# A U stage in 512-column matmuls, gelu's last product on GpSimd, and expert lists made by one-hot products

## The chip, the cores and the metric

The kernel runs on one core of one Trainium2 chip. The metric is the device time of one execution in microseconds (us). The kernel before took 2601.82 us, the median of three runs (2600.1 to 2602.65). Engines are named as in the profile: PE is TensorE, DVE is VectorE, ACT is ScalarE, POOL is GpSimd, SP issues most loads.

## The reference

Two transformer blocks run one after the other on 256 tokens of width 2048, in float32. The change touches the first block's expert layer alone, which looks up experts by product keys:

```python
v1, i1 = lax.top_k(s1, 16)                    # scores of 128 keys, for 8 heads, two sides
v2, i2 = lax.top_k(s2, 16)
vs, ci = lax.top_k(v1[..., :, None] + v2[..., None, :], 16)
eidx = e1 * 128 + e2                          # 128 of 16384 experts for each token
gates = softmax(vs)
act = gelu(einsum('tkd,td->tk', expert_u[eidx], x))
out = einsum('tk,tkd->td', act * gates, expert_v[eidx])
```

`expert_u` and `expert_v` are 16384 x 2048 each.

## The kernel before

It is one program, unrolled, in which each engine takes its instructions in the order in which they are written; semaphores between engines come from the use of the tiles. A stream of steps feeds PE (`Stream`); each step has a `prep` (load, split, one step ahead: `la = 1`) and an `mm` (its matmuls). Beside it runs a list of generators, the background: after each step it may spend a budget (2.2 a step, and 2.0 from step 64 on), and each `yield` of a generator says what its piece costs. So the place of background work in each engine's queue is set by these numbers.

A float32 product with nearly full precision is made of three products of a faster type, fp32r: an operand is split into a high part (a copy on ACT) and a low part (a subtraction, source minus high part, on DVE), and high x high, high x low and low x high are summed in PSUM.

*U stage (128 steps, lines 776 to 851).* Step f takes 128 experts and computes their products with all 256 tokens, whether a token chose them or not. Their rows of `expert_u` are loaded, transposed in blocks on DVE (`turn`, L808), and used as weights against x, held transposed in sixteen blocks k of 128 rows: `xt["h"]` and `xt["l"]`, the high and low parts, with 256 columns (tokens) each. In steps 0 to 63 the blocks k = 0 to 7 are done as plain float32 products (L829, weights `uT`, moving `xf`), which come first in the step, and k = 8 to 15 in three fp32r products of 256 columns each (L834, L835, L836); from step 64 on all sixteen blocks are done in three. The high parts are made by ACT at L818, the low parts by DVE at L823, in tiles of 1024 columns, four of each kind.

The result is 128 experts x 256 tokens in PSUM. gelu without its half (which lies in the gates) follows: Square on ACT (L839), a product on DVE (L840), and one step later, in `u_finish`, Tanh on ACT (L849), a product with the PSUM values on DVE (L850), and the write to the DRAM table `AG` from GpSimd's queue (L851).

*Background of the U stage.* The scores and the two rounds of top-k (DVE, about steps 3 to 21, 31 to 41 and 51 to 67), the gates of each token as products of two one-hot matrices (PE, ACT and DVE, L1048 to L1065), which GpSimd's queue writes into the other half of `AG` (L1082), and `lists_gen`. That sorts the 16384 experts into four classes: chosen in the first 128 tokens only, in both halves, in the second half only, in none. It computes the place of each expert in the sorted list, as integers `posU`, and then 128 indirect DMAs on GpSimd write the expert numbers to these places of a DRAM table `listD` (L1121, each with a small memset behind it, five in a yield of 2.0). The table is read back, transposed by PE (L1134) and copied to `listI` (L1135).

*V stage.* Steps of 128 list entries gather rows of `AG` and of `expert_v` by `listI` (L872, L873), multiply activations and gates, split both and multiply on PE (L896 to L898), for one or both halves of the tokens. Where the classes begin and end in steps is fixed by `WA, WB0, WB1`: the blocks from WB0 to WA count for both halves. A flag is set where the classes don't fit these bounds; then further blocks run behind a branch.

Of the kernel before, what the change touches and what calls it, by code (L numbers as in the profile page):

```python
# [12 lines left out]
F32 = mybir.dt.float32  # L13
# [5 lines left out]
OP = mybir.AluOpType  # L19
# [10 lines left out]
WA, WB0, WB1 = 82, 27, 111  # L30
# [59 lines left out]
def tile_kernel(ctx: ExitStack, tc: tile.TileContext, A, out, dbg=None):  # L90
# [20 lines left out]
    def bank(tag):  # L111
        return psp.tile([128, 512], F32, tag=tag, name=tag)
# [156 lines left out]

    def new_xt():  # L270
        xt["h"] = xp.tile([128, 16, 256], F32R, tag="xh", name="xh")
        xt["l"] = xp.tile([128, 16, 256], F32R, tag="xl", name="xl")
# [30 lines left out]
    def flat(t):  # L303
        return t.rearrange("p a b -> p (a b)")
# [446 lines left out]
    listD = dr.tile([NE * 128, 64], F32, name="listD")  # L751
# [10 lines left out]
    r_bc = tk.tile([128, 256], F32, name="r_bc")  # L762
# [17 lines left out]
    gap = tk.tile([1, 1], F32, name="gap")  # L780
# [6 lines left out]
    class UStep:  # L787
# [23 lines left out]
        def prep(self):  # L811
            if self.uT is None:
                self.turn()
            n = (16 - self.nf) * 128 // self.nw
            self.u = []
            for i in range(self.nw):
                hi, lo = wh_tile()[:, :n], wl_tile()[:, :n]
                S.activation(hi, self.uT[:, self.nf * 128 + i * n:self.nf * 128 + (i + 1) * n], AF.Copy)  # L818
                self.u.append((hi, lo))
            if self.f + 1 < NE:  # L820
                steps[self.f + 1].turn()
            for i, (hi, lo) in enumerate(self.u):
                V.tensor_tensor(lo, self.uT[:, self.nf * 128 + i * n:self.nf * 128 + (i + 1) * n], hi.bitcast(F32),  # L823
                                op=OP.subtract)

        def mm(self):
            acc = ubank[self.f % 3][:, 0:256]
            for k in range(self.nf):
                T.matmul(acc, self.uT[:, k * 128:(k + 1) * 128], xf[:, k, :], start=(k == 0), stop=False)  # L829
            per = (16 - self.nf) // self.nw  # L830
# [14 lines left out]
    def u_finish():  # L845
        if not pend:
            return
        f, x, a = pend.pop()
        S.activation(a, a, AF.Tanh, scale=GC3)  # L849
        V.scalar_tensor_tensor(a, a, 1.0, x, op0=OP.add, op1=OP.mult)  # L850
        G.dma_start(AG[f * 128:f * 128 + 128, 0:256], a)  # L851

    class VStep:
# [12 lines left out]
        def prep(self):  # L866
# [12 lines left out]
            for c in range(2):  # L879
                if self.rest:  # L880
                    hi, lo = [xt[n].rearrange("p k t -> p (k t)")[:, c * 1024:(c + 1) * 1024] for n in "hl"]
# [203 lines left out]
    def lists_gen():  # L1085
# [27 lines left out]
        V.tensor_copy(posU, pf[:, 0:128])  # L1113
# [6 lines left out]
        for f in range(NE):  # L1120
            i = G.indirect_dma_start(out=listD[:, :], out_offset=bass.IndirectOffsetOnAxis(ap=posU[:, f:f + 1], axis=0),  # L1121
                                     in_=idf[:, f:f + 64], in_offset=None)
            tc.declare_no_dep(i.ins, group="list", reason="the rows written are all different")
            tc.add_to_no_dep_group("list", i.ins)
# [422 lines left out]
    def merged_gen(i, j0, j1):  # L1547
        for j in range(j0, j1):
# [7 lines left out]
            split(flat(xt["h"][:, k0:k0 + 2, :]), flat(xt["l"][:, k0:k0 + 2, :]), pt)  # L1556
# [39 lines left out]
```

## Time and profile before

| | us |
|---|---|
| median of three runs | 2601.82 |
| the profiled execution's own time | 2613.04 |
| its span, first to last instruction | 2611.3 |
| U stage, first to last U matmul | 391.3 to 1343.7 |
| of it, lists and scatters | 1076.4 to 1343.7 |
| first V product | 1357.29 |

The span is what the views below cover; the time has a little around it. The page's busy shares are means over all stages, so what an engine does in one stage is read from windows.

### The profile page before, as it was taken

How to read it: one execution, taken by the hardware profiler on the slowest of the kernel's cores; microseconds unless marked ns; L12 is line 12 of the kernel's file. 1: busy time of each engine (PE TensorE's matmuls, PEld its weight loads, DVE VectorE, ACT ScalarE, POOL GpSimd, SP SyncE). 2: the span in 40 equal slices, each digit the busy share in tenths (PEclk: the TensorE clock that was granted, in tenths of full speed). 3: DMA queues.
4: the chain of work that ended last, by engine and by line, in shares of the span. 5: the costliest groups of instructions: out<-in, count | busy, mean ns of one | idle time of the engine just before them, and what ended most of it. 6: DMA issues, size and time to landing. Idle time of an engine off the chain costs nothing. (4 is left out here: it accounts for less than half of the span.)

```text
span 2611.3 us, 38031 instructions
## 1 busy us (share of the span) xinstructions
PE 2516.7 (96%) x13895; PEld 2195.1 (84%) x13896; DVE 1815.7 (70%) x2804; ACT 1315.0 (50%) x2169; POOL 554.3 (21%) x789
## 2 busy tenths in 40 slices
PE   9999989999999999998779999999999999999999
PEld 8877779899898999997668888887888888888887
DVE  5665678987979989886447777777665456754564
ACT  6764643254452577543235555555555456544443
POOL 3000000001201112388725555553000000000000
PEclk9999999999999999999789999999999999999999
DMA  6644876565757868696469989987555545555554
GB/s 220 193 129 146 193 165 167 165 168 168 220 144 201 212 176 223 181 241 192 127 241 324 320 321 318 320 317 273 189 191 187 184 163 180 190 178 193 181 193 157
DMA packets 251619, 538.63 MB, mean 206 GB/s; under 512 B 29800, under 2 KB 165952, under 8 KB 236832
## 3 DMA queue, kind: packets, MB, share of 16 engines
q1 hardware_dynamic: 206864, 344.54, 44.4%
q0 software_dynamic: 40992, 189.67, 21.2%
q10 hardware_dynamic: 3568, 1.91, 0.3%
q8 instruction: 111, 1.82, 0.3%
q14 instruction: 84, 0.69, 0.1%
HBM read 494.06 MB, written 41.94 MB: 205 GB/s over the span
## 5 line engine op out<-in xcount | busy, mean ns | idle before, releaser
L120 DVE TENSOR_TENSOR wl<-raw,wh 128x1024 fp32r<-128x1024 f32 (+4 forms) x642 | 740.3, 1171 | 375.8 <-ACT wh L119 341.3
L119 ACT ACTIVATE wh<-raw 128x1024 fp32r<-128x1024 f32 (+4 forms) x642 | 640.1, 1011 | 372.2 <-PE acc L247 279.0
L836 PE MATMUL acc<-xh,wl 128*128 128x256 f32 x1536 | 444.7, 289 | 31.0 <-DVE wl L823 20.7
L245 PE MATMUL acc<-wh,xh 128*128 128x512 f32 (+2 forms) x1152 | 456.7, 396 | 6.0 <-ACT h L406 4.2
L834 PE MATMUL acc<-xh,wh 128*128 128x256 f32 x1536 | 456.0, 297 | 6.1 <-issue 5.5
L835 PE MATMUL acc<-xl,wh 128*128 128x256 f32 x1536 | 441.6, 288 | 9.3 <-issue 8.5
L247 PE MATMUL acc<-wh,xl 128*128 128x512 f32 (+2 forms) x1152 | 447.3, 388 | 0.0
L246 PE MATMUL acc<-wl,xh 128*128 128x512 f32 (+2 forms) x1152 | 446.6, 388 | 0.3 <-DVE wl L120 0.3
L808 DVE STREAM_TRANSPOSE uT<-raw 128x2048 f32<-128x2048 f32 x128 | 295.4, 2308 | 60.5 <-PE acc L829 54.0
L836 PEld LDWEIGHTS acc<-xh,wl 128*128 128x128 f32 x1536 | 300.5, 196 | 39.2 <-DVE wl L823 26.0
L835 PEld LDWEIGHTS acc<-xl,wh 128*128 128x128 f32 x1536 | 301.2, 196 | 11.9 <-issue 10.2
L834 PEld LDWEIGHTS acc<-xh,wh 128*128 128x128 f32 x1536 | 300.9, 196 | 11.8 <-issue 9.9
L245 PEld LDWEIGHTS acc<-wh,xh 128*128 128x128 f32 x1152 | 217.5, 189 | 47.3 <-ACT h L406 4.6
L839 ACT ACTIVATE ga<-acc 128x256 f32<-128x256 f32 x128 | 49.1, 383 | 412.3 <-PE acc L836 325.0
L247 PEld LDWEIGHTS acc<-wh,xl 128*128 128x128 f32 x1152 | 217.3, 189 | 44.0
L246 PEld LDWEIGHTS acc<-wl,xh 128*128 128x128 f32 x1152 | 217.8, 189 | 41.0 <-DVE wl L120 0.7
L818 ACT ACTIVATE wh<-uT 128x1024 fp32r<-128x1024 f32 x192 | 195.1, 1049 | 87.3 <-DVE uT L808 87.2
L829 PE MATMUL acc<-xf,uT 128*128 128x256 f32 x1024 | 234.3, 382 | 3.9 <-ACT h L404 3.9
L823 DVE TENSOR_TENSOR wl<-uT,wh 128x1024 fp32r<-128x1024 f32 x192 | 224.6, 1197 | 7.6 <-ACT wh L818 7.5
L851 POOL DMA_DIRECT2D AG<-ga x128 | 71.1, 556 | 739.4 <-DVE ga L850 723.7
L829 PEld LDWEIGHTS acc<-xf,uT 128*128 128x128 f32 x1024 | 190.9, 191 | 28.2 <-ACT h L404 4.3
L872 POOL DMA_INDIRECT ag<-AG,listI x111 | 142.5, 1284 | 75.9 <-DVE pl L120 51.6
(418 smaller groups left out, 3817.4 us busy)
## 6 DMA issues: line engine op xcount, KB each, us to landing
raw<-in_expert_u_dram SPq DMA_DIRECT2D x1024, 128.0 KB
raw<-in_w_in_dram SPq DMA_DIRECT2D x96, 1024.0 KB
raw<-in_w_out_dram SPq DMA_DIRECT2D x32, 1024.0 KB
raw<-in_w_pq_dram SPq DMA_DIRECT2D x64, 256.0 KB
AG<-ga POOLq DMA_DIRECT2D x128, 128.0 KB
AG<-GB POOLq DMA_DIRECT2D x64, 256.0 KB
raw<-in_w_ple_gate_dram SPq DMA_DIRECT2D x16, 1024.0 KB
raw<-in_w_in_dram SPq DMA_DIRECT2D x16, 544.0 KB
```

What stands on the lines that cost most here:

```text
L119: S.activation(hi, src, AF.Copy)
L120: V.tensor_tensor(lo, src, hi.bitcast(F32), op=OP.subtract)
L245: T.matmul(o, xh, hi, start=first, stop=False)
L246: T.matmul(o, xh, lo, start=False, stop=False)
L247: T.matmul(o, xl, hi, start=False, stop=last)
L808: V.transpose(uT.rearrange("p b g j -> p g b j"), self.raw.rearrange("p g (b i) -> p g b i", i=32))
L818: S.activation(hi, self.uT[:, self.nf * 128 + i * n:self.nf * 128 + (i + 1) * n], AF.Copy)
L823: V.tensor_tensor(lo, self.uT[:, self.nf * 128 + i * n:self.nf * 128 + (i + 1) * n], hi.bitcast(F32), op=OP.subtract)
L829: T.matmul(acc, self.uT[:, k * 128:(k + 1) * 128], xf[:, k, :], start=(k == 0), stop=False)
L834: T.matmul(acc, hi[:, c], xt["h"][:, k, :], start=(k == 0), stop=False)
L835: T.matmul(acc, hi[:, c], xt["l"][:, k, :], start=False, stop=False)
L836: T.matmul(acc, lo[:, c], xt["h"][:, k, :], start=False, stop=(k == 15))
```

## The change

It has four parts.

1. *U in 512 columns.* The tiles `xh` and `xl` no longer hold the high and the low parts, but the blocks 0 to 7 and 8 to 15, each with high and low part side by side. One matmul of 512 columns then multiplies a high weight block with both; its bank holds two sums, which a copy on ACT and an add on DVE put together. The order within a step is: all high blocks but the last, the float32 blocks, the low blocks, the last high block.
2. *GpSimd* subtracts the last quarter of a step's low parts, and makes gelu's last step, an add of 1 and a product, in SBUF.
3. *The lists* are made without DRAM: the list is a sum, over 128 groups of 128 experts, of products of two one-hot matrices (low seven bits of the place against high seven bits, with the expert's number as the value), in 16 groups of eight. A few small products make the part of the number that the group contributes.
4. `WA, WB0, WB1` go from 82, 27, 111 to 81, 28, 110. The pool `t1` has seven buffers instead of five; `r_bc` lies in the pool `g2`.

PE at the start of the U stage. Names on the left of the arrow are outputs; `wh` and `wl` are high and low weights. Before:

```order
L829 MATMUL acc<-xf,uT 128x256 x8
L834 MATMUL acc<-xh,wh 128x256
L835 MATMUL acc<-xl,wh 128x256
L836 MATMUL acc<-xh,wl 128x256
L834 MATMUL acc<-xh,wh 128x256
```

and now (x8 joins the last high block of one step with the seven first ones of the next):

```order
L846 MATMUL acc<-xl,wh 128x512 x7
L852 MATMUL acc<-xf,uT 128x256 x8
L854 MATMUL acc<-xl,wl 128x256 x8
L846 MATMUL acc<-xl,wh 128x512 x8
L852 MATMUL acc<-xf,uT 128x256 x8
```

The float32 blocks and the low blocks have moved behind the high ones.

DVE in a U step of the first half, with a piece of top-k (`oh`, `e`) behind it. Before:

```order
L808 STREAM_TRANSPOSE uT<-raw 128x4x16x32
L823 TENSOR_TENSOR wl<-uT,wh 128x1024
L850 SCALAR_TENSOR_TENSOR ga<-ga,acc 128x256
L840 SCALAR_TENSOR_TENSOR ga<-ga,acc 128x256
L1017 TENSOR_TENSOR oh<-rf,iota 128x512
L1019 TENSOR_TENSOR oh<-oh,i_2672 128x512
```

and now:

```order
L814 STREAM_TRANSPOSE uT<-raw 128x4x16x32
L834 TENSOR_TENSOR wl<-uT,wh 128x768
L859 TENSOR_TENSOR gx<-acc,gx 128x256
L862 SCALAR_TENSOR_TENSOR ga<-ga,gx 128x256
L1041 TENSOR_TENSOR oh<-rf,iota 128x512
L1043 TENSOR_TENSOR oh<-oh,i_2672 128x512
```

The product for the step before (L850) is gone from DVE; the add (L859) stands directly ahead of the product (L862) that takes the square of the add's result, `ga`, from ACT.

GpSimd where the lists are made. Before:

```order
L1125 MEMSET gap 1x1
L851 DMA AG<-ga 128x256
L1082 DMA AG<-GB 128x8x64
L1121 DMA listD<-idf,posU 16384x64
L1125 MEMSET gap 1x1
```

and now:

```order
L1106 DMA AG<-GB 128x8x64
L828 TENSOR_TENSOR wl<-uT,wh 128x512
L872 TENSOR_SCALAR ga<-ga 128x256
L873 TENSOR_TENSOR ga<-ga,gx 128x256
L874 DMA AG<-ga 128x256
```

The scatters are gone, and each step has three operations of arithmetic ahead of its write.

The diff, cut to its core:

```diff
-WA, WB0, WB1 = 82, 27, 111
+WA, WB0, WB1 = 81, 28, 110
...
     def new_xt():
-        xt["h"] = xp.tile([128, 16, 256], F32R, tag="xh", name="xh")
-        xt["l"] = xp.tile([128, 16, 256], F32R, tag="xl", name="xl")
+        xt["x"] = [xp.tile([128, 8, 2, 256], F32R, tag=t, name=t) for t in ("xh", "xl")]
+        xt["h"], xt["l"] = Half(xt["x"], 0), Half(xt["x"], 1)
...
     def t1(dt, name):
-        return tk.tile([128, 256], dt, tag="t1", name=name, bufs=5)
+        return tk.tile([128, 256], dt, tag="t1", name=name, bufs=7)
...
                 S.activation(hi, self.uT[:, self.nf * 128 + i * n:self.nf * 128 + (i + 1) * n], AF.Copy)
                 self.u.append((hi, lo))
+            q = n * (4 - self.nw) // 4
+            hi, lo = self.u[-1]
+            G.tensor_tensor(lo[:, q:], self.uT[:, 2048 - n + q:], hi[:, q:].bitcast(F32), op=OP.subtract)
             if self.f + 1 < NE:
                 steps[self.f + 1].turn()
             for i, (hi, lo) in enumerate(self.u):
-                V.tensor_tensor(lo, self.uT[:, self.nf * 128 + i * n:self.nf * 128 + (i + 1) * n], hi.bitcast(F32),
-                                op=OP.subtract)
+                src = self.uT[:, self.nf * 128 + i * n:self.nf * 128 + (i + 1) * n]
+                m = n if i + 1 < self.nw else n * (4 - self.nw) // 4
+                V.tensor_tensor(lo[:, :m], src[:, :m], hi[:, :m].bitcast(F32), op=OP.subtract)
 
         def mm(self):
-            acc = ubank[self.f % 3][:, 0:256]
+            bank = ubank[self.f % 3]
+            acc = bank[:, 0:256]
...
+            def high(k):
+                T.matmul(bank, part(k, 0), xt["x"][k // 8][:, k % 8].rearrange("p n t -> p (n t)"),
+                         start=(k == self.nf), stop=(k == 15))
+
+            for k in range(self.nf, 15):
+                high(k)
             for k in range(self.nf):
-                T.matmul(acc, self.uT[:, k * 128:(k + 1) * 128], xf[:, k, :], start=(k == 0), stop=False)
...
+                T.matmul(acc, self.uT[:, k * 128:(k + 1) * 128], xf[:, k, :], start=False, stop=False)
             for k in range(self.nf, 16):
-                hi, lo = self.u[(k - self.nf) // per]
-                c = slice((k - self.nf) % per * 128, ((k - self.nf) % per + 1) * 128)
-                T.matmul(acc, hi[:, c], xt["h"][:, k, :], start=(k == 0), stop=False)
-                T.matmul(acc, hi[:, c], xt["l"][:, k, :], start=False, stop=False)
-                T.matmul(acc, lo[:, c], xt["h"][:, k, :], start=False, stop=(k == 15))
+                T.matmul(acc, part(k, 1), xt["h"][:, k, :], start=False, stop=False)
+            high(15)
             u_finish()
+            u = t1(F32, "gx")
+            S.activation(u, bank[:, 256:512], AF.Copy)
+            V.tensor_tensor(u, acc, u, op=OP.add)
             a = t1(F32, "ga")
-            S.activation(a, acc, AF.Square)
-            V.scalar_tensor_tensor(a, a, GC1 / GC3, acc, op0=OP.add, op1=OP.mult)
-            pend.append((self.f, acc, a))
+            S.activation(a, u, AF.Square)
+            V.scalar_tensor_tensor(a, a, GC1 / GC3, u, op0=OP.add, op1=OP.mult)
+            pend.append((self.f, u, a))
...
         S.activation(a, a, AF.Tanh, scale=GC3)
-        V.scalar_tensor_tensor(a, a, 1.0, x, op0=OP.add, op1=OP.mult)
+        G.tensor_scalar(a, a, 1.0, None, op0=OP.add)
+        G.tensor_tensor(a, a, u, op=OP.mult)
         G.dma_start(AG[f * 128:f * 128 + 128, 0:256], a)
...
         yield 3.0
-        for f in range(NE):
-            i = G.indirect_dma_start(out=listD[:, :], out_offset=bass.IndirectOffsetOnAxis(ap=posU[:, f:f + 1], axis=0),
-                                     in_=idf[:, f:f + 64], in_offset=None)
...
-            G.memset(gap, 0.0)
-            if f % 5 == 4:
-                yield 2.0
-        lt = t1(F32, "lt")
-        G.dma_start(GB, listD.rearrange("(b p) o -> b p o", p=128))
-        for _ in range(4):
-            yield 2.0
-        V.tensor_copy(lt[:, 0:128], GB[:, :, 0])
-        pt = bank("ms")
-        T.transpose(pt[:, 0:128], lt[:, 0:128], ident)
-        V.tensor_copy(listI, pt[:, 0:128])
...
+        def hots(tag, col, n):
+            o = tk.tile([128, 8, 128], BF16, tag=tag, name=tag, bufs=3)
+            V.tensor_tensor(o[:, 0:n], iotaf[:, None, :].to_broadcast([128, n, 128]),
+                            pq[:, col:col + n][:, :, None].to_broadcast([128, n, 128]), op=OP.is_equal)
+            return o
...
+        def products(f0, oa, ob):
+            for j in range(8):
+                T.matmul(lst, ob[:, j], oa[:, j], start=(f0 + j == 0), stop=(f0 + j == NE - 1))
+
+        for f0 in range(0, NE, 8):
+            oa, ob = hots("o1", f0, 8), hots("o2", 128 + f0, 8)
+            S.activation(flat(oa), flat(oa), AF.Copy, scale=pcol)
+            if prev:
+                products(*prev)
+            prev = (f0, oa, ob)
+            yield 2.3
+        products(*prev)
+        V.scalar_tensor_tensor(hf[:, 0:128], hf[:, 128:256], 128.0, lst, op0=OP.mult, op1=OP.add)
+        V.tensor_copy(listI, hf[:, 0:128])
         yield
```

Left out are the class `Half`, which gives the old indexing of `xt["h"]` and `xt["l"]`, the small products of part 3 ahead of the groups (yields of 4.0, 4.0, 1.0 and 2.0), and two places that index the new tiles.

## Rows read from the trace of the kernel before

**Rows 1.** The page, part 1: busy us (share of the span) xinstructions.
```profile
PE 2516.7 (96%) x13895; PEld 2195.1 (84%) x13896; DVE 1815.7 (70%) x2804; ACT 1315.0 (50%) x2169; POOL 554.3 (21%) x789
```

**Rows 2.** Windows: stretch, length, busy of PE, PEld, DVE, ACT, POOL, clock, DMA, GB/s.
```profile
460.00:520.00 60.00, 54.64 (x338) 49.81 (x337) 58.13 (x111) 16.35 (x26) 4.89 (x9) 1.00 0.59 164
...
1076.40:1169.40 93.00, 88.70 (x731) 87.56 (x732) 82.11 (x92) 39.43 (x61) 69.49 (x113) 1.00 0.85 224
1169.40:1210.70 41.30, 36.86 (x290) 36.11 (x288) 29.11 (x29) 15.49 (x24) 35.69 (x58) 0.96 0.79 219
1210.70:1290.50 79.80, 55.95 (x290) 48.21 (x290) 33.60 (x33) 15.48 (x24) 61.58 (x113) 0.76 0.43 121
1290.50:1319.30 28.80, 28.80 (x241) 28.62 (x239) 27.39 (x27) 12.91 (x20) 12.60 (x22) 1.00 0.92 289
1319.30:1343.70 24.40, 14.44 (x102) 14.25 (x101) 5.06 (x10) 3.98 (x8) 1.62 (x3) 0.79 0.41 152
...
1440.00:1500.00 60.00, 60.00 (x264) 49.24 (x263) 42.93 (x59) 33.57 (x44) 32.99 (x29) 1.00 0.90 321
```

**Rows 3.** Waits of PE, 1076 to 1344: us in total, times, longest.
```profile
PE ms L1134 <- DVE lt L1132: 9.9, 1, 9.9
PE acc L836 <- issue: 9.7, 15, 2.4
PE acc L835 <- issue: 8.5, 14, 1.1
PE acc L834 <- issue: 5.5, 11, 1.0
PE acc L836 <- DVE wl L823: 4.3, 4, 1.7
PE ms L1101 <- DVE cls L1095: 2.5, 1, 2.5
```

**Rows 4.** Groups: xcount, busy us, mean ns, idle before and its releaser.
```profile
L1121 POOL DMA_INDIRECT listD<-idf,posU x128 | 136.4, 1066 | 30.4 <-issue 30.4
...
L1017 DVE TENSOR_TENSOR oh<-rf,iota 128x512 f32<-128x512 f32 x16 | 11.0, 685 | 0.2
```

**Rows 5.** Timeline of PE, two U steps: start us, us, engine, line.
```profile
444.50 3.62 PE L829 MATMUL acc<-xf,uT 128*128 128x256 f32 x16
...
448.08 0.28 PE L835 MATMUL acc<-xl,wh 128*128 128x256 f32 x1
...
450.83 3.62 PE L829 MATMUL acc<-xf,uT 128*128 128x256 f32 x16
```

**Rows 6.** Timeline of PE in the V stage, 36 matmuls apart.
```profile
1399.67 0.39 PE L896 MATMUL ms<-wh,ph 128*128 128x512 f32 x1
...
1407.91 0.39 PE L896 MATMUL ms<-wh,ph 128*128 128x512 f32 x1
```

**Rows 7.** Timeline of PE, four bf16 products of the gates.
```profile
903.96 0.39 PE L1060 MATMUL acc<-o,o 128*128 128x128 bf16 x4
```

**Rows 8.** Timeline of DVE in a top-k stretch.
```profile
500.41 2.30 DVE L808 STREAM_TRANSPOSE uT<-raw 128x2048 f32<-128x2048 f32 x1
502.64 1.18 DVE L823 TENSOR_TENSOR wl<-uT,wh 128x1024 fp32r<-128x1024 f32 x1
503.74 0.41 DVE L850 SCALAR_TENSOR_TENSOR ga<-ga,acc 128x256 f32<-128x256 f32 x1
504.07 0.41 DVE L840 SCALAR_TENSOR_TENSOR ga<-ga,acc 128x256 f32<-128x256 f32 x1
```

**Rows 9.** Timeline of the last U step's gelu and the first V product.
```profile
1344.11 0.42 DVE L840 SCALAR_TENSOR_TENSOR ga<-ga,acc 128x256 f32<-128x256 f32 x1 [4.52 <-ACT ga L839]
1344.57 0.42 ACT L849 ACTIVATE ga<-ga 128x256 f32<-128x256 f32 x1 [0.49 <-DVE ga L840]
1345.02 0.42 DVE L850 SCALAR_TENSOR_TENSOR ga<-ga,acc 128x256 f32<-128x256 f32 x1 [0.48 <-ACT ga L849]
...
1357.29 0.51 PE L896 MATMUL acc<-wh,ph 128*128 128x512 f32 x1 [2.91 <-ACT wh L119]
```

**Rows 10.** Timeline of POOL and DVE near the program's start.
```profile
24.61 0.46 POOL L444 TENSOR_TENSOR band<-band,ident 128x128 f32<-128x128 f32 x1
...
25.29 1.57 DVE L120 TENSOR_TENSOR wl<-raw,wh 128x384 fp32r<-128x384 f32 x2 [1.50 <-ACT wh L119]
...
26.09 1.09 POOL L444 TENSOR_TENSOR band<-band,ident 128x128 f32<-128x128 f32 x1
```

More of the change, by code (lines that the diff above doesn't have):

```diff
@@ L779, in tile_kernel @@
     flagI = tk.tile([1, 1], I32, name="flagI")
-    gap = tk.tile([1, 1], F32, name="gap")
     ubank = [bank("acc") for _ in range(3)]
@@ L828, in mm, with part @@
+            acc = bank[:, 0:256]
+            per = (16 - self.nf) // self.nw
+            def part(k, n):
+                c = (k - self.nf) % per * 128
+                return self.u[(k - self.nf) // per][n][:, c:c + 128]
+            def high(k):
[3 more added lines that the diff above has]
+                high(k)
             for k in range(self.nf):
-                T.matmul(acc, self.uT[:, k * 128:(k + 1) * 128], xf[:, k, :], start=(k == 0), stop=False)
@@ L880, in prep @@
                 if self.rest:
-                    hi, lo = [xt[n].rearrange("p k t -> p (k t)")[:, c * 1024:(c + 1) * 1024] for n in "hl"]
+                    both = xt["x"][0].rearrange("p k n t -> p (k n t)")
+                    hi, lo = [both[:, c * 2048 + j * 1024:c * 2048 + j * 1024 + 1024] for j in range(2)]
                 else:
@@ L1129, in lists_gen @@
-        G.dma_start(GB, listD.rearrange("(b p) o -> b p o", p=128))
-        for _ in range(4):
-            yield 2.0
-        V.tensor_copy(lt[:, 0:128], GB[:, :, 0])
-        pt = bank("ms")
-        T.transpose(pt[:, 0:128], lt[:, 0:128], ident)
-        V.tensor_copy(listI, pt[:, 0:128])
+        tz = t1(BF16, "tz")
+        V.memset(tz[:, 0:3], 0.0)
+        V.tensor_copy(tz[:, 3:7], tot[:, 0:4])
+        st = bank("ms")
+        T.matmul(st[:, 0:4], wt[:, 384:512], tz[:, 3:7], start=True, stop=False)
@@ new lines, in lists_gen @@
+        for c in range(3):
+            T.matmul(st[:, 0:4], wt[:, 512:640], tz[:, 2 - c:6 - c], start=False, stop=(c == 2))
+        pq = g2([128, 264], name="pq")
+        both = g2([128, 264], U32, "pu")
+        V.tensor_copy(both[:, 0:128], pf[:, 0:128])
+        V.tensor_copy(both[:, 128:132], st[:, 0:4])
+        V.tensor_scalar(posU[:, 0], both[:, 0:128], 7, None, op0=OP.logical_shift_right)
+        V.tensor_scalar(posU[:, 1], both[:, 0:128], 127, None, op0=OP.bitwise_and)
+        V.tensor_scalar(both[:, 136:140], both[:, 128:132], 7, None, op0=OP.logical_shift_right)
@@ new lines, in lists_gen @@
+        V.tensor_scalar(both[:, 140:144], both[:, 128:132], 127, None, op0=OP.bitwise_and)
+        V.tensor_copy(pq[:, 0:256], flat(posU))
+        V.tensor_copy(pq[:, 256:264], both[:, 136:144])
+        yield 4.0
+        def hots(tag, col, n):
[3 more added lines that the diff above has]
+            return o
@@ new lines, in lists_gen @@
+        tri = t1(F32, "tri")
+        V.tensor_scalar(tri[:, 0:128], iotaf, pcol, None, op0=OP.is_ge)
+        V.tensor_scalar(tri[:, 128:256], iotaf, pcol, None, op0=OP.is_gt)
+        oa, ob = hots("o1", 256, 4), hots("o2", 260, 4)
+        sp = bank("ms")
+        for c in range(4):
+            T.matmul(sp[:, 0:128], ob[:, c], oa[:, c], start=(c == 0), stop=(c == 3))
+        ss = t1(F32, "st")
+        V.memset(ss[:, 128:129], 1.0)
+        S.activation(ss[:, 0:128], sp[:, 0:128], AF.Copy)
@@ new lines, in lists_gen @@
+        yield 4.0
+        sc = bank("ms")
+        T.matmul(sc[:, 0:1], ss[:, 0:128], ss[:, 128:129], start=True, stop=True)
+        V.tensor_copy(ss[:, 129:130], sc[:, 0:1])
+        yield 1.0
+        sr = bank("ms")
+        T.matmul(sr[:, 0:128], tri[:, 0:128], ss[:, 0:128], start=True, stop=False)
+        T.matmul(sr[:, 0:128], ss[:, 129:130].to_broadcast([128, 128]), tri[:, 128:256], start=False, stop=True)
+        hiU = t1(U32, "hu")
+        hf = t1(F32, "hf")
+        V.tensor_scalar(hf[:, 0:128], sr[:, 0:128], 127.0, None, op0=OP.add)
@@ L1555, in merged_gen @@
             k0 = 8 * i + 2 * j
-            split(flat(xt["h"][:, k0:k0 + 2, :]), flat(xt["l"][:, k0:k0 + 2, :]), pt)
+            split(xt["h"][:, k0:k0 + 2, :], xt["l"][:, k0:k0 + 2, :], pt.rearrange("p (a b) -> p a b", a=2))
             yield
```

27 lines of the change are left out of this document (17 added, 10 removed).

## The prediction

> **What bounds the kernel now.** I began with the page's totals: PE is busy for 2516.7 of 2611.3 us [rows 1], so time can be won only by giving PE less to do or by filling the 95 us in which it stands still. Then I took the stages as a table of windows [rows 2]. The reader is to see three kinds of stretch there. In the V stage (1440 to 1500) PE is busy for 60.00 of 60 us: matmuls alone count. In the top-k stretches of the U stage (460 to 520 lies in one) PE has 54.64 of 60 and DVE 58.13 of 60: there DVE is the bound, and PE waits for it. From 1076.4 on the lists are made, and everything is slower: between 1210.7 and 1290.5 PE is busy for 55.95 of 79.8 us, at a granted clock of 0.76, a mix of the levels of 2.4 and 1.2 GHz; DVE, ACT and POOL have room there, and DMA is at 0.43.
>
> Third, the waits of PE from 1076 to 1344 [rows 3]: 23.7 us (9.7, 8.5 and 5.5) go to "issue", where nothing that the profile shows was missing, and 9.9 us to the one transpose that waits for the list to come back from DRAM. The first kind appears only while GpSimd issues its 128 scatters [rows 4]; PE is back at a busy share of 1 as soon as they are done (1290.5 to 1319.3) [rows 2]. That the scatters cause it is an inference from this coincidence; the profile names no releaser.
>
> How long a U step takes without any wait comes from two timelines. With eight f32 blocks, step to step is 450.83 - 444.50 = 6.33 us, and the 24 matmuls of 256 columns in it come 2.75 / 23 = 0.120 us apart [rows 5]. A step with all sixteen blocks split takes 48 such matmuls, 5.74 us. Matmuls of 512 columns of the same type come (1407.91 - 1399.67) / 36 = 0.229 us apart [rows 6].
>
> **The change, part by part.**
>
> *U in 512 columns.* Two matmuls of 256 columns become one of 512: 0.239 becomes 0.229, 0.010 us a pair. There are 64 x 8 + 64 x 16 = 1536 pairs: -16 us. The number of weight loads falls by a third, but they were hidden; the columns streamed stay the same. The f32 products cost what they did.
>
> *The lists.* Steps 94 to 127 last from 1076.4 to 1343.7, 267.3 us [rows 2]. Their own matmuls are 34 x 5.74 = 195 us, so 72 us are extra: 34 us of the waits above, some 8 of small waits [rows 3], and 30 of matmuls at the low clock. All that hangs on the scatters goes. What comes: 128 products of bf16, 128 columns each. Four such begin at 903.96 and take 0.39 us [rows 7], between 0.055 (if their drains overlap) and 0.098 apiece; with 0.08 that is 10 us, and 3 us for the small products. Three of the small ones stand right behind DVE work of their own, and PE takes its queue in order, so the next U step waits behind them: each time for the 1.2 us of add, square and product that stand ahead on DVE, and 0.3 to 1.9 us of that work, 7 us in all; with the 3 us that the first list products wait already [rows 3] it is 10 us. The sixteen groups need two comparisons of 1024 columns each on DVE. One of 512 columns takes 0.685 us [rows 4], so 1.15 us each in sequence, 2.3 a group. A group costs 2.3 of a budget of 2.0 a step, so 16 groups stretch over 18 steps, 2.0 us a step on DVE. DVE's own work in such a step is 2.23 of transpose, 1.65 of low parts, 1.2 of add, wait and product (below), 5.1 us; with 2.0 it is 7.1, against 5.58 (16 x 0.229 + 16 x 0.120) + 0.65 of PE. DVE is the bound by 0.87 us for 18 steps: 16 us, less some 4 that the later use of the low parts hides once, plus 5 for GpSimd in the way (below). Sum 40 us in place of 72: -32.
>
> *The waits in DVE's queue.* Until now DVE ran two products back to back, 504.07 - 503.74 = 0.33 us apart, the first of them for the step before [rows 8]. Now the add stands directly ahead of the product that needs the square of its sum, and ACT makes that square. The same round trip stands at the end of the U stage: DVE at 1344.11, ACT at 1344.57, DVE again at 1345.02, 0.91 us [rows 9]. So DVE stands for some 0.5 us in every step where it is behind. Against it: a quarter of the low parts goes, 1.10 / 4 = 0.27 us [rows 8]. Per step 1.76 becomes 0.83 + 0.91 + 0.33 = 2.07, say +0.27 us. Where PE is the bound this costs nothing. In the top-k stretches, 17, 10 and 17 steps, it is paid each time: 44 x 0.27 = +12 us.
>
> *GpSimd.* A step now gives it the low parts (256 or 512 columns), an add, a product and the write of AG. Its only two-input rows are 128 x 128: 0.46 us undisturbed, 1.09 at worst [rows 10]. By these, 512 columns lie between 1.3 and 4.4 us, 256 between 0.7 and 2.2. I take the row without disturbance with its start-up counted once, 1.3 and 0.75: with the add and the write 3 to 4 us a step, below 5.58. PE needs GpSimd's quarter only near the end of the next step, so it is hidden until GpSimd needs more than a step. At the worst row, 4.4 + 2.2 + 1.1 + 0.6, it would, by 2.7 us a step.
>
> The worst row has a reason that reaches DVE: at 26.09 GpSimd's product runs inside DVE's pair of subtractions that began at 25.29, and takes 1.09 in place of 0.46 [rows 10]. The Trainium skill's page "SBUF — State Buffer", section "Who interferes with whom", says why: a DVE instruction with two SBUF inputs and a GpSimd instruction that reads SBUF exclude each other, and whichever began first holds the port to its end. The trace agrees for GpSimd's side. By that rule DVE would pay as often as GpSimd does; that is the slower rival below. From the rows alone DVE's share is between nothing and 0.63 us (1.09 - 0.46) for each clash. I take 0.1 us a step, near nothing, since the rows show GpSimd as the one that waits: 44 steps, +4 us (those of the lists are counted above).
>
> *Small ones.* In the gate steps with sixteen split blocks ACT gets one more copy and a wait for DVE inside its queue; its slack is thin: +3 us. At the end of U the chain to AG grows by a copy, an add and GpSimd's two operations in place of DVE's one. V starts at 1357.29, 12 us after that chain [rows 9], with the projection's matmuls between; +2 us. Loads, buffers of t1 (seven for two tiles a step) and the transposes that now wait for f32 products later in a step have slack of more than a step: nothing.
>
> *V stage.* 81, 28 and 110 give 53 blocks for both token parts and 57 for one, 163 units in place of 166. Each is 12 matmuls of 0.229: -8 us, PE being the bound without a gap [rows 2]. It needs the experts to fit: the reference's inputs select 10216 in the first token part (at most 10368), 3730 of them only there (at least 3584), and 13965 in all (at most 14080). They fit.
>
> **The sum.** -16 - 32 + 12 + 4 + 3 + 2 - 8 = -35 us. The profiled execution took 2613.0 us, so 2578 for one like it. The runs shown have a median of 2601.8, 11 us less; I take the difference from the median, 2567 us. If the 11 us sit in the stalls of the list stage, which the profiled execution would then show too long, the gain is 24 us, 2578.
>
> **The rivals.**
>
> *The lists are free, the DVE wait too.* If the low parts' later use gives PE enough slack to ride over DVE's peaks, the list stage costs 18 in place of 40 and the top-k stretches stay as they are: 2567 - 22 - 12 = 2533. For it: every product of low parts now stands behind all the high ones. Against it: the slack helps once in a stretch, and DVE's sum per step is above PE's for 18 steps in a row.
>
> *The stalls were the profile's.* 2578, as above. For it: nothing but the 11 us. Against it: the 9.9 us wait is a DMA round trip that every execution has.
>
> *GpSimd and DVE lock each other out (slower).* The place is the shared reading of SBUF in all U steps in which DVE is near the bound: 44 of top-k, 34 of lists, 29 with gates. The price is up to 0.63 us a step for DVE, in place of 0.1. The gain is gone at 35 / 107 = 0.33 us more a step; at 0.63 it is 107 x 0.53 = 57 us more, 2624. For it: the 1.09 us row, and 4.1 of DVE's 7.1 us in a list step are two-input work. Against it: those rows show the lengthening on GpSimd.
>
> *The counts do not fit.* Then 93 blocks run one after the other behind the branch, each at least the 2.75 us of its matmuls and mostly a DMA round trip: over 250 us more. The counts above speak against it.
>
> **How the numbers follow.** Forecast (2550 to 2591) 0.55; all hidden 0.15; the profile's stalls (2570 to 2597) 0.18; GpSimd and DVE 0.11; counts 0.01. The range 2536 to 2602 leaves out the fast tail of the second and the greater part of the fourth. A change of 0.2%, 5.2 us, is about what can be told from none: faster than 2596.6 are the first two, most of the third and a little of the fourth, 0.86; within it 0.06; slower 0.08.
>
> **What would show it.** Right: 512-column U matmuls 0.229 us apart; no "issue" waits after 1076 and a clock of 1 there; in top-k stretches DVE idle about 0.5 us a step before the second product, by ACT; PE waiting in list steps for low parts or one-hots; V shorter by 8 us. Wrong: low parts of DVE longer than 1.2 us while GpSimd reads; PE waiting for GpSimd; list steps at 5.6 us, which would mean that DVE was not the bound; stalls by "issue" that stay without any scatter.

## The result: 76 us slower, and the profile after

The changed kernel takes 2677.49 us (median of four runs, 2674.99 to 2678.69), the kernel before 2601.45; the ratio is 1.0291, with an interval of 1.0273 to 1.0309. Forecast were 2567, and at most 2602.

The page, part 1, of the changed kernel, as in [rows 1]:

```profile
PE 2534.7 (95%) x12465; PEld 2113.1 (79%) x12465; DVE 1904.8 (71%) x2851; ACT 1367.5 (51%) x2311; POOL 769.6 (29%) x913
```

PE has fewer instructions, as intended, but the span has grown from 2611.3 to 2676.6 us, so PE stands still for 142 us in place of 95. Where, the windows tell, in the columns of [rows 2] (top-k, gates, lists, V):

```profile
460.00:520.00 60.00, 52.89 (x254) 42.83 (x254) 53.60 (x114) 15.56 (x32) 23.55 (x32) 1.00 0.56 156
...
1064.06:1090.69 26.63, 23.56 (x158) 20.63 (x157) 23.98 (x36) 20.09 (x47) 12.46 (x13) 1.00 0.52 137
1231.81:1348.21 116.40, 96.92 (x538) 80.36 (x537) 109.28 (x96) 54.24 (x83) 69.09 (x65) 0.91 0.59 161
1500.00:1560.00 60.00, 60.00 (x259) 48.24 (x258) 43.71 (x58) 33.80 (x44) 27.32 (x29) 1.00 0.89 312
```

In the top-k stretch DVE is busy for 53.60 us where it had 58.13: it is still the bound, but it idles. In the V stage nothing is missing. The step times, read from one copy out of a step's bank (ACT) to the next, say how much each stretch of the U stage has lost. "Before, again" is a second profile of the kernel before (below):

| steps | before | before, again | after | after less before, again |
|---|---|---|---|---|
| 0 to 5 | 38.8 | 38.8 | 48.4 | +9.6 |
| top-k: 5 to 22, 32 to 42, 51 to 64 | 275.8 | 275.9 | 301.3 | +25.4 |
| gates, first half: 22 to 32, 42 to 51 | 156.5 | 156.5 | 153.4 | -3.1 |
| gates, second half: 64 to 93 | 205.6 | 205.6 | 240.3 | +34.7 |
| lists: 93 to 127 | 267.3 | 257.7 | 264.0 | +6.3 |
| all | 944.1 | 934.5 | 1007.6 | +73.1 |

The two longest waits of PE in the list stage (1141 to 1405), to compare with [rows 3]. No row of "issue" is left; the granted clock, which the prediction expected at 1, is 0.91 in the third row above:

```profile
PE acc L1198 <- ACT o L1202: 16.0, 12, 1.9
PE acc L846 <- ACT wh L824: 9.1, 19, 1.4
```

The waits of ACT from 390 to 1405, its longest row:

```profile
ACT ga L861 <- DVE gx L859: 420.4, 126, 8.0
```

and of DVE:

```profile
DVE ga L862 <- ACT ga L861: 67.6, 127, 0.8
```

In the mean of a step ACT stands for 3.3 us at Square (L861) until DVE has added (L859), and DVE for 0.53 us at the product (L862) until Square is done. DVE in a top-k step:

```profile
486.74 0.92 DVE L834 TENSOR_TENSOR wl<-uT,wh 128x768 fp32r<-128x768 f32 x1
...
488.53 0.43 DVE L862 SCALAR_TENSOR_TENSOR ga<-ga,gx 128x256 f32<-128x256 f32 x1 [0.55 <-ACT ga L861]
488.87 0.29 DVE L1005 MAX8 v<-h 128x8 f32<-128x128 f32 x1
```

From the low parts to the next piece of top-k it is 2.13 us, where it was 1.76 [rows 8]. The groups of DVE's low parts, by shape (busy us, mean ns):

```profile
L834 DVE TENSOR_TENSOR wl<-uT,wh 128x1024 fp32r<-128x1024 f32 x64 | 104.5, 1634 | 4.6 <-ACT wh L824 4.6
L834 DVE TENSOR_TENSOR wl<-uT,wh 128x512 fp32r<-128x512 f32 x64 | 79.9, 1248 | 0.0
...
L834 DVE TENSOR_TENSOR wl<-uT,wh 128x768 fp32r<-128x768 f32 x64 | 59.0, 921 | 0.0
```

768 columns take 0.92 us in the first half; 512 take 1.25 in the mean of the second, and more in the gate steps from 1064 to 1091:

```profile
L834 DVE TENSOR_TENSOR wl<-uT,wh 128x512 fp32r<-128x512 f32 x4 | 7.1, 1783 | 0.0
```

That is waiting, not work: GpSimd subtracts its quarter there at the same time, and where it does not, the same 512 columns take 0.68 us (they end the 1.78 us in the run with Square later, below).

Two steps show how this closes into a ring. ACT in a gate step (start us, us, engine, line):

```profile
970.77 0.42 ACT L861 ACTIVATE ga<-gx 128x256 f32<-128x256 f32 x1 [1.87 <-DVE gx L859]
...
975.72 2.00 ACT L824 ACTIVATE wh<-uT 128x1024 fp32r<-128x1024 f32 x2
...
980.15 0.42 ACT L861 ACTIVATE ga<-gx 128x256 f32<-128x256 f32 x1 [1.86 <-DVE gx L859]
```

DVE in the same step:

```profile
974.14 2.30 DVE L814 STREAM_TRANSPOSE uT<-raw 128x2048 f32<-128x2048 f32 x1
976.79 2.93 DVE L834 TENSOR_TENSOR wl<-uT,wh 128x1024 fp32r<-128x1024 f32 x2 [0.36 <-ACT wh L824]
979.64 0.41 DVE L859 TENSOR_TENSOR gx<-acc,gx 128x256 f32<-128x256 f32 x1
980.60 0.94 DVE L862 SCALAR_TENSOR_TENSOR ga<-ga,gx 128x256 f32<-128x256 f32 x1 [0.54 <-ACT ga L861]
```

GpSimd, and PE:

```profile
977.81 1.37 POOL L828 TENSOR_TENSOR wl<-uT,wh 128x512 fp32r<-128x512 f32 x1 [5.01 <-ACT wh L824]
```

```profile
976.81 2.12 PE L846 MATMUL acc<-xh,wh 128*128 128x512 f32 x8 [1.87 <-ACT wh L824]
```

Follow it round. Square runs at 970.77. Behind it in ACT's queue stands gate work for 4.6 us, and only then the high parts (975.72). Their first half is the signal for three: PE (976.81), DVE's low parts (976.79), and, with the second half, GpSimd's quarter (977.81). DVE's add stands behind those low parts (979.64), and Square of the next step behind the add (980.15). Once round is 9.38 us, and that is the step; PE has work for 7.9. Since high parts now come late, DVE and GpSimd begin on nearly the same signal: GpSimd's quarter starts 0.12 us ahead of DVE's last 512 columns (977.93), and DVE's 1536 columns take 2.93 us.

A list step, DVE:

```profile
1243.48 0.41 DVE L859 TENSOR_TENSOR gx<-acc,gx 128x256 f32<-128x256 f32 x1
1244.37 0.43 DVE L862 SCALAR_TENSOR_TENSOR ga<-ga,gx 128x256 f32<-128x256 f32 x1 [0.49 <-ACT ga L861]
1244.72 2.35 DVE L1164 TENSOR_TENSOR o<-iotaf,pq 128x1024 bf16<-128x1024 f32 x2
1246.99 2.30 DVE L814 STREAM_TRANSPOSE uT<-raw 128x2048 f32<-128x2048 f32 x1
1249.22 3.05 DVE L834 TENSOR_TENSOR wl<-uT,wh 128x1024 fp32r<-128x1024 f32 x2
1252.19 0.41 DVE L859 TENSOR_TENSOR gx<-acc,gx 128x256 f32<-128x256 f32 x1
```

Here DVE alone is the bound: 0.41 + 0.48 idle + 0.35 + 2.27 + 2.23 + 2.97 = 8.71 us, add to add. The prediction had 7.1.

### The profile page after: what moved, and what is told of

It reads as the page before. It is cut to its first block, busy times and chain, and to the rows that moved or that the text cites. A ratio compares the mean times of both kernels' runs of the same rounds, so it can differ in the third digit from the quotient of the medians.

```text
span 2676.6 us, 35551 instructions
## 1 busy us (share of the span) xinstructions
PE 2534.7 (95%) x12465; PEld 2113.1 (79%) x12465; DVE 1904.8 (71%) x2851; ACT 1367.5 (51%) x2311; POOL 769.6 (29%) x913
## 5 line engine op out<-in xcount | busy, mean ns | idle before, releaser
L846 PE MATMUL acc<-xl,wh 128*128 128x512 f32 x1024 | 288.2, 406 | 13.5 <-ACT wh L824 9.6
L828 POOL TENSOR_TENSOR wl<-uT,wh 128x256 fp32r<-128x256 f32 (+1 forms) x128 | 138.4, 1082 | 537.0 <-ACT wh L824 536.9
L861 ACT ACTIVATE ga<-gx 128x256 f32<-128x256 f32 x128 | 53.5, 418 | 423.1 <-DVE gx L859 421.0
L834 DVE TENSOR_TENSOR wl<-uT,wh 128x1024 fp32r<-128x1024 f32 (+1 forms) x192 | 238.4, 1268 | 4.6 <-ACT wh L824 4.6
L245 PE MATMUL acc<-wh,xh 128*128 128x512 f32 (+1 forms) x576 | 230.6, 400 | 5.8 <-ACT h L416 4.0
L245 PE MATMUL acc<-wh,xl 128*128 128x512 f32 (+1 forms) x576 | 225.5, 391 | 0.0
L246 PE MATMUL acc<-wl,xh 128*128 128x512 f32 (+1 forms) x576 | 223.8, 389 | 0.4 <-DVE wl L120 0.3
L247 PE MATMUL acc<-wh,xh 128*128 128x512 f32 (+1 forms) x576 | 224.0, 389 | 0.0
L247 PE MATMUL acc<-wh,xl 128*128 128x512 f32 (+1 forms) x576 | 222.6, 386 | 0.0
L246 PE MATMUL acc<-wl,xl 128*128 128x512 f32 (+1 forms) x576 | 222.4, 386 | 0.0
L846 PE MATMUL acc<-xh,wh 128*128 128x512 f32 x512 | 152.1, 445 | 24.6 <-ACT wh L824 24.5
L854 PE MATMUL acc<-xl,wl 128*128 128x256 f32 x1024 | 153.7, 293 | 20.7 <-DVE wl L834 20.6
L872 POOL TENSOR_SCALAR ga<-ga 128x256 f32<-128x256 f32 x128 | 156.6, 1224 | 0.1
```

Source lines behind the costliest of these rows:

```text
L245: T.matmul(o, xh, hi, start=first, stop=False)
L246: T.matmul(o, xh, lo, start=False, stop=False)
L247: T.matmul(o, xl, hi, start=False, stop=last)
L834: V.tensor_tensor(lo[:, :m], src[:, :m], hi[:, :m].bitcast(F32), op=OP.subtract)
L846: T.matmul(bank, part(k, 0), xt["x"][k // 8][:, k % 8].rearrange("p n t -> p (n t)"), start=(k == self.nf), stop=(k == 15))
L854: T.matmul(acc, part(k, 1), xt["h"][:, k, :], start=False, stop=False)
```

## The experiments

Each ratio is to the kernel before, timed in the same session (its medians lie between 2602.5 and 2604.3 us), with a 95% interval. Differences from the changed kernel are taken from its 2677.49 us. A group is one of the sixteen groups of the lists; the ring is the round trip described above, and the lock is GpSimd and DVE holding each other up.

**Lists alone.** The kernel before with parts 3 and 4 of the change.

> The kernel before with the lists by one-hot products and the new class bounds alone; U steps, gelu and low parts as before. Three theories for the loss of 76 us. Ring: in the changed U step Square waits on ACT for DVE's add, the add stands behind DVE's low parts, and ACT makes the next high parts only behind Square, so ACT and DVE go round in a ring. Lock: GpSimd's quarter of the low parts holds DVE's low parts up (2.5 to 3.05 us for 1536 columns). Lists: the one-hot lists themselves make the steps of 8.7 us. By ring or lock the loss lies in the parts that are left out here: list steps of at most 7.4 us (transpose 2.2, low parts 2.2, two products 0.66, one-hots 2.35), lists and V together win 30 to 40 us on before: 2560 to 2570. By the third theory the list steps stay at 8.7 us and the time is 2585 or more.

2581.47 us, 0.9911 (0.9894 to 0.9928). DVE in a list step:

```profile
1190.58 2.39 DVE L1136 TENSOR_TENSOR o<-iotaf,pq 128x1024 bf16<-128x1024 f32 x2
1192.85 2.34 DVE L804 STREAM_TRANSPOSE uT<-raw 128x2048 f32<-128x2048 f32 x1
1195.08 2.35 DVE L819 TENSOR_TENSOR wl<-uT,wh 128x1024 fp32r<-128x1024 f32 x2
1197.31 0.45 DVE L846 SCALAR_TENSOR_TENSOR ga<-ga,acc 128x256 f32<-128x256 f32 x1
1197.64 0.45 DVE L836 SCALAR_TENSOR_TENSOR ga<-ga,acc 128x256 f32<-128x256 f32 x1
1197.97 2.39 DVE L1136 TENSOR_TENSOR o<-iotaf,pq 128x1024 bf16<-128x1024 f32 x2
```

A step is 7.39 us, and 2048 columns of low parts take less than 1536 beside GpSimd. Steps 93 to 127 take 235.0 us, 39 over PE's 195.8. The time is 11 us above the expected range: the stalls of [rows 3] do not come in every execution, and the new bounds win nothing in the profile of the V stage (both below). Against the second profile of the kernel before, the U steps are 22.6 us shorter (911.9 against 934.5), which is about the 21 us that the times show. The loss lies in parts 1 and 2.

**Square later, low parts on DVE, and both.** Square and the product behind it move to the end of the next step (the tanh moves with them); or GpSimd's quarter goes back to DVE. The kernels with a later Square or product also have eight buffers of `t1` in place of seven, and take the sixteen columns of `iota` out of `iotaf`:

```diff
             u_finish()
             u = t1(F32, "gx")
             S.activation(u, bank[:, 256:512], AF.Copy)
             V.tensor_tensor(u, acc, u, op=OP.add)
-            a = t1(F32, "ga")
-            S.activation(a, u, AF.Square)
-            V.scalar_tensor_tensor(a, a, GC1 / GC3, u, op0=OP.add, op1=OP.mult)
-            pend.append((self.f, u, a))
+            pend.append([self.f, u, None])    # u_finish of the next step makes both
```

```diff
-            G.tensor_tensor(lo[:, q:], self.uT[:, 2048 - n + q:], hi[:, q:].bitcast(F32), op=OP.subtract)
...
-                m = n if i + 1 < self.nw else n * (4 - self.nw) // 4
+                m = n
```

> The changed kernel with Square and the product behind it one step later, so that no instruction on ACT waits for an add of DVE in the same step. Ring: gate steps fall from a mean of 8.9 us to about 8.1 (DVE's own work), list steps with a group from 8.7 to 8.2, DVE's idle 0.5 us a step goes: 40 to 55 us less, 2622 to 2637. Lock: only the 0.5 us of idle time in the steps where DVE is the bound go, 15 to 25 us less, 2652 to 2662; gate steps stay above 8.5.

2601.12 us, 0.9993 (0.9984 to 1.0003): 76 us less than the changed kernel, the whole loss and more than either theory had. ACT in a gate step:

```profile
1031.96 1.99 ACT L823 ACTIVATE wh<-uT 128x1024 fp32r<-128x1024 f32 x2
1033.86 0.40 ACT L866 ACTIVATE ga<-ga 128x256 f32<-128x256 f32 x1
1034.16 0.40 ACT L873 ACTIVATE ga<-gx 128x256 f32<-128x256 f32 x1
1034.98 0.38 ACT L857 ACTIVATE gx<-acc 128x256 f32<-128x256 f32 x1 [0.41 <-PE acc L845]
```

and DVE:

```profile
1032.28 3.19 DVE L1073 TENSOR_SCALAR o<-iotaf,eT,gT 128x128 f32<-128x128 f32 x8
...
1037.62 1.78 DVE L833 TENSOR_TENSOR wl<-uT,wh 128x1024 fp32r<-128x1024 f32 x2
```

In this step nothing on ACT waits for DVE, the step is PE's 7.93 us, and the 1536 columns take 1.78 us although GpSimd still has its quarter: the two no longer begin together. GpSimd's quarter (1034.04 to 1035.39) now meets DVE's one-hots, whose eight take 3.19 us, where those of the next step (1039.99) take 2.14; where PE is the bound, that costs nothing. In the list steps the two still begin together, and 1536 columns take 3.05 us there.

> The changed kernel with all low parts on DVE; GpSimd keeps only gelu's add and product. Lock: the low parts of a step with sixteen split blocks take 2.4 us for 2048 columns in place of 2.9 for 1536, or less than they take now in all; gate and list steps lose 0.5 to 1.1 us each, top-k steps gain 0.25: 20 to 45 us less, 2632 to 2657. Ring alone: the ring is as long as the low parts on DVE are, which without a lock grow by 0.25 to 0.6 us a step: 10 to 30 us more, 2687 to 2707.

2663.75 us, 1.023 (1.0213 to 1.0247): 14 us less than the changed kernel, between the two forecasts. 

> Both edits together. If ring and lock are two causes, they add up: gate steps 7.5 us (PE's own work), list steps with a group 7.9, top-k steps 0.24 us over those of before where DVE is the bound: some 75 us less than the changed kernel, about 2600. If one of them is the whole cause, this is no better than the better one of the two before it, 2625 to 2640.

2594.27 us, 0.9961 (0.9947 to 0.9975). Once Square is later, GpSimd's quarter costs 7 us: 3.2 in steps 64 to 93 (206.8 us with it, 203.6 without) and 3.9 in the list steps 98 to 121 (170.0 with it, 166.1 without, 156.9 with the lists alone).

**Square on DVE.** `V.tensor_tensor(a, u, u, op=OP.mult)` in place of ACT's Square.

> The changed kernel with the square made by DVE (a product of u with itself) in place of ACT, in the same place of the order. DVE gets 0.4 us more a step and loses its idle 0.5; ACT no longer waits for DVE's add. Ring: the loss goes as with the later Square, gate steps fall from a mean of 8.9 to about 8.1 us, 2600 to 2620. If what counts is only DVE's own time a step, nothing changes: 2670 to 2685.

2681.22 us, 1.0297 (1.0274 to 1.0321): nothing gained, and the ring as the only cause is refuted. DVE in a list step:

```profile
1271.56 3.06 DVE L834 TENSOR_TENSOR wl<-uT,wh 128x1024 fp32r<-128x1024 f32 x2
1274.54 0.41 DVE L859 TENSOR_TENSOR gx<-acc,gx 128x256 f32<-128x256 f32 x1
1274.98 0.64 DVE L861 TENSOR_TENSOR ga<-gx 128x256 f32<-128x256 f32 x1
1275.66 0.43 DVE L862 SCALAR_TENSOR_TENSOR ga<-ga,gx 128x256 f32<-128x256 f32 x1
```

The idle 0.5 us has become 0.7 us of work, and DVE is as long as before. The stretches differ, though: steps 64 to 93 fall from 240.3 to 225.4 us, the top-k steps rise from 301.3 to 316.2. The gate steps do not come down to the 206.8 of the later Square: GpSimd's quarter meets DVE's one-hots there, whose eight take 3.4 to 3.8 us in many steps in place of 2.13, so this run does not part the ring from the lock.

**The product alone later.** Square stays, so that ACT still waits; only L862 moves to the next step, so that DVE doesn't:

```diff
+            S.activation(a, u, AF.Square)
+            pend.append([self.f, u, a, False])
...                                            # in u_finish, for the step before:
+            V.scalar_tensor_tensor(p[2], p[2], GC1 / GC3, p[1], op0=OP.add, op1=OP.mult)
```

> The changed kernel with Square where it is, so that ACT still waits for DVE's add ahead of the next high parts, but with the product behind it one step later, so that DVE no longer waits for ACT. This parts the two halves of the later Square. DVE's own time: idle time of 0.5 us a step is gone, and with it most of the loss, 2600 to 2620; ACT's waits for the add stay at 3 us a step. Ring: the high parts are as late as before and the loss stays, 2655 to 2680. If both count, the top-k and list stretches recover (by 0.5 us a step) and the gate stretch, where ACT has 5 us of gate work between Square and the high parts, does not: 2620 to 2640.

2650.65 us, 1.0189 (1.0172 to 1.0206): of the 76 us, 27 are back. By stretches it is the third case: top-k 277.6 us (301.3 after, 280.7 with Square later), steps 64 to 93 239.3 (240.3, 206.8). DVE there:

```profile
1068.75 2.30 DVE L813 STREAM_TRANSPOSE uT<-raw 128x2048 f32<-128x2048 f32 x1
1072.34 2.91 DVE L833 TENSOR_TENSOR wl<-uT,wh 128x1024 fp32r<-128x1024 f32 x2 [1.29 <-ACT wh L823]
1075.17 0.61 DVE L875 SCALAR_TENSOR_TENSOR ga<-ga,gx 128x256 f32<-128x256 f32 x1
1075.70 0.41 DVE L858 TENSOR_TENSOR gx<-acc,gx 128x256 f32<-128x256 f32 x1
```

DVE now idles 1.29 us for high parts that are no earlier; round the ring, in which the moved product (0.53 us) now stands ahead of the add, it is 9.84 us. So both halves count: DVE's idle time in the top-k and list steps, the ring in the gate steps, where ACT has its gate work between Square and the high parts. The split into 27 and 49 us is not clean, because the moved product makes the ring longer than the 9.38 us it had. The eighth buffer of `t1` is in this kernel too, so it is not what the later Square gained by.

**No arithmetic on GpSimd**, with Square in its place and later: all low parts on DVE, and gelu's end as one product there.

> The changed kernel with neither low parts nor gelu's last product on GpSimd: DVE makes all low parts and the last product as one instruction. The idle 0.5 us between add and second product stays. The run with the square on DVE gained nothing although ACT no longer waited, so the ring is not the whole cause; what is left is that DVE's own time a step is too long, made up of work, idle time and lengthening by GpSimd. If the lengthening counts as the trace has it (the 512-column low part takes 1.68 us in place of some 0.6), gate steps fall by 0.7 to 1 us, list steps with a group by 0.4, and the top-k steps pay 0.6 more: 2655 to 2675. If GpSimd's lengthening is hidden, only the added work is left: 2695 to 2715.

2672.28 us, 1.0267 (1.025 to 1.0284). Steps 64 to 93 fall to 225.9 us, top-k rises to 314.2: GpSimd takes about as much from DVE as it gives. 

> The same with Square and second product one step later, so that DVE neither idles nor is lengthened; U in 512 columns, DVE's add and the lists by products are all that is left of the change. DVE's time a step with a group: transpose 2.23, low parts 2.35, add 0.33, two products 0.66, one-hots 2.25, 7.8 us, against 7.4 with the lists alone: 2590 to 2600, above the 2581.5 of the lists alone. If U in 512 columns pays as the prediction had it (16 us of PE), it is below that, 2565 to 2575.

2595.46 us, 0.9974 (0.9963 to 0.9984), the same as with gelu's end on GpSimd (2594.27). What U in 512 columns leaves over the lists alone is a loss of 14 us. It lies in the top-k steps, where DVE is the bound: 288.4 us against 274.7, or 0.34 us in each of 40 steps, the length of DVE's add (0.33). The gate steps win 4.4 us.

**Class bounds alone, and before once more.**

> The kernel before with the class bounds 81, 28 and 110 alone. The prediction counted 8 us less for three units of twelve matmuls, 2594. In every kernel run so far with these bounds the V stage is as long as before (465 to 468 us), because its matmuls come 0.2333 us apart in place of 0.229. If the bounds bring that pitch with them, nothing is won: 2601 to 2604 and a pitch of 0.233. If something else does (the number of t1 buffers, say), the 8 us are there: 2592 to 2596 and a pitch of 0.229.

2595.02 us, 0.9964 (0.9953 to 0.9976). 

> The kernel before once more, for its profile alone. Two questions. Are the stalls by issue in the list stage, 23.7 us in its first profile, the same in each execution? With the class bounds alone changed they were gone in the profile. If they vary, this span is another than 2611.3, and part of the 72 us that the prediction took from the list stage was that execution's. And is the pitch of 0.229 us of the V products its own? If the class bounds make the pitch of 0.233, it is 0.229 again here.

Span 2604.8. Its waits of PE in the list stage:

```profile
PE acc L836 <- DVE wl L823: 17.7, 8, 2.4
PE ms L1134 <- DVE lt L1132: 17.5, 1, 17.5
```

The stalls by "issue" of [rows 3] are gone, with all 128 scatters; in their place PE waits longer for the list to come back. The stage is 10 us shorter (257.7 against 267.3), not 24: from the first scatter's start to the last one's it is 211.5 us here and 214.5 in the first profile, so the scatters last about as long without the stalls. What sets their pace was not tested. The 24 us of stalls stand in one of the three profiles that have the scatters. Two V products of this profile, 36 apart:

```profile
1439.62 0.39 PE L897 MATMUL acc<-wl,ph 128*128 128x512 f32 x1
...
1447.86 0.39 PE L897 MATMUL acc<-wl,ph 128*128 128x512 f32 x1
```

and of the kernel with the new bounds alone:

```profile
1439.77 0.40 PE L898 MATMUL ms<-wh,pl 128*128 128x512 f32 x1
...
1448.17 0.40 PE L898 MATMUL ms<-wh,pl 128*128 128x512 f32 x1
```

The pitch, the time from one such matmul to the next, is 0.229 and 0.233 us. In both profiles with the old bounds it is the first, in all fourteen with the new ones 0.233, or 0.234 where `t1` has eight buffers, so the three units less win nothing in the profiles: from the first V product to the end 1256.2 us (before, again) and 1255.9. Yet the timed runs are 8.5 us faster. They spread from 2590.6 to 2601.7, and the profiled one was the slowest of ten; where the 8.5 us lie, and why the pitch changes, stays open.

**Variants of the lists.** Five t1 buffers; groups spread; bf16 inputs; float32 blocks in steps 103 to 121.

> The lists by one-hot products and the new bounds as in the run of the lists alone, but with five t1 buffers in place of seven, as in the kernel before. If the number of these buffers (they hold the weights of the V products) makes the slower pitch in the V stage, the pitch returns to 0.229 us and the time to 2571 to 2575. If not, 2579 to 2584 and a pitch of 0.233. The U stage does not change in either case.

2582.19 us, 0.9914 (0.9891 to 0.9936), pitch 0.233: the buffers are not it. 

> As the lists alone with five t1 buffers, with the sixteen groups spread over 21 steps in place of 18 (each counted 2.6 of a budget of 2.0) and the reading of p ahead of the lists. A step with a group is bound by DVE at 7.4 us, one without by PE at 5.76: DVE's sum over the stretch does not fall, but the steps without a group give it room. 2 to 6 us less than that run. If the steps with a group stay at 7.4 and those without do not absorb anything, the same time as that run.

2585.52 us, 0.9925 (0.9903 to 0.9948): no gain over 2582.19. 

> The lists alone (as in the first run), with bf16 inputs for the one-hots: one of each pair as one comparison of 1024 columns of bf16, the other as eight comparisons of 128 columns with a scalar per partition. In that run DVE was the bound of a step with a group, 7.4 us, 2.25 of it one-hots in float32; PE needs 6.4. If bf16 inputs shorten either form, the step falls towards PE's 6.4: 2565 to 2576. If both forms take as long as before, 2580 to 2584.

2584.88 us, 0.9933 (0.9916 to 0.9949). One comparison of 1024 columns takes 1.21 us from bf16 and 1.25 from float32, and with the other of each pair as eight narrow comparisons a step with a group takes 7.57 us in place of 7.40:

```profile
L1143 DVE TENSOR_TENSOR o<-iotab,pqb 128x1024 bf16<-128x1024 bf16 x16 | 19.4, 1212 | 0.0
```

> The lists alone (as in the first run), with steps 103 to 121 in the form of the first 64 steps, eight float32 blocks and eight split ones. PE gets 0.57 us more a step and DVE's low parts halve, 1.1 us less: a step with a group is then bound by PE at 6.33 + 0.64 = 7.0 us in place of DVE's 7.4, one without a group takes 6.33 in place of 6.26. If DVE's sum was the bound, 4 to 7 us less than 2581.5; if PE's queue was already the bound, 6 to 10 us more.

2577.67 us, 0.9912 (0.9895 to 0.9928). Windows of 120 us in the list stage, of this kernel:

```profile
1090.00:1210.00 120.00, 116.23 (x865) 110.92 (x865) 106.22 (x109) 44.96 (x69) 21.53 (x31) 1.00 0.74 204
```

and of the lists alone:

```profile
1090.00:1210.00 120.00, 110.03 (x937) 107.81 (x936) 115.70 (x117) 54.69 (x79) 20.09 (x29) 1.00 0.74 201
```

DVE is relieved, PE is the bound, a group step takes 6.84 in place of 7.40. Over all steps it gives 3.6 us; the timed runs of the two overlap. The five kernels with the lists and the old U step (lists alone and the four variants) beat both kernels, by 18 to 25 us against the kernel before.

## Why the prediction was wrong

*U in 512 columns, -16.* The size holds where PE is the bound: 6.25 in place of 6.33 us and 5.57 in place of 5.76. There are few such steps left, and DVE's add costs more in the others. Even with the waits gone, parts 1 and 2 cost 20 us over the lists alone (2601.12 against 2581.47), where the prediction had -16 and +4.

*The lists, -32.* By themselves they cost 39 us over PE's work, and I had 40; that is luck in part, since the 40 counted the add, the wait and 5 us for GpSimd, none of which is in the kernel with the lists alone. Two things failed. The 72 us to be saved were 62 in the second profile (257.7 - 195.8), so the rival "the stalls were the profile's" was partly right. That PE is full again "as soon as they are done" was also misread: in the first profile eight scatters start between 1294.9 and 1305.2, in a stretch in which PE has no gap. And beside parts 1 and 2 a group step takes 8.71 us, not 7.1: low parts 2.97 in place of 1.65, and the one-hots 2.27 in place of the 2.0 of an average step.

*The waits in DVE's queue, +12: the step that failed.* "Where PE is the bound this costs nothing" and "44 x 0.27" counted DVE's half of the round trip alone, and only in steps in which DVE was the bound before. (By its own numbers that half is 2.07 - 1.76 = 0.31, not 0.27; in the top-k step at 486.74 it is 2.13 - 1.76 = 0.37.) ACT's half (it stands at Square until the add, which stands behind the low parts) was put under "small ones" at +3. So the two terms came to +15, and what they stand for was worth 76: that is what the later Square, which takes both halves away, gave back (with GpSimd's part in the ring, below). Parting them gave 27 us to the first, and left 49 to the second. The top-k steps lost 25 us, of which the 0.37 us in 40 steps make 15; steps 64 to 93 lost 35. In the first steps 10 more went: PE waits there 6.0 us for copies of the queries on ACT (two waits from 400 to 460; before, 0.5), and one such copy begins at 422.27, right behind a Square that waited 2.07 us for DVE.

*GpSimd, +4.* DVE's share was taken at 0.1 us a clash, "near nothing"; it is 1.2 us in a gate step (2.93 less 1.78) and as much in a list step. The sign named for a wrong forecast, low parts over 1.2 us while GpSimd reads, is there. In [rows 10] GpSimd was the one that waited; DVE's second subtraction had begun 0.11 us before it. The Trainium skill's rule ("SBUF — State Buffer", "Who interferes with whom"), that whichever begins first holds the port to its end, is borne out for DVE's side too: in the gate step at 977.81 GpSimd began 0.12 us ahead, and DVE's 512 columns took 1.78 us in place of 0.68. The rival's mechanism was there, at about twice the 0.63 us a step that it was given, but what it cost in time hung on the ring: GpSimd's quarter costs 14 us with Square in its place and 7 with Square later.

*V, -8.* Nothing in the profiles, by the pitch of 0.233. *End of U, +2.* From the last copy to the first V product it is 17.0 us, in place of 13.6 in the first profile of the kernel before and 14.2 in the second.

## What to carry over

An instruction that waits for another engine holds up all that stands behind it in its queue: before adding one, list what is behind it on both engines and go round until you come back. If you do come back, the length of the round trip, background work included, is a lower bound for the step. The remedy is to issue the waiting instruction one step later. Here it took one more buffer, and about 1 us at the end of the U stage (18.1 us from the last copy to the first V product, in place of 17.0).

## What the runs showed of the hardware

GpSimd's subtraction of 512 columns takes 1.27 us, its product of 256 0.74, its add of a constant to 256 0.84, and 1.82 beside DVE's low parts in the list steps. DVE's eight one-hots of 128 columns (L1073), with one tensor input, rose from 2.13 us to between 3.4 and 3.8 beside GpSimd in many steps of the run with the square on DVE. With the same 128 scatters, PE showed 24 us of waits by "issue" in one execution and none in another. And the same V products came 0.229 or 0.233 us apart where the class bounds alone differed, at a granted clock of 1.00 in both; the runs do not show why.
